# Moving the homes of a decoder trunk's buffers to multiples of 256 bytes

## The chip, the cores and the metric

The kernel runs on one core of a Trainium2 chip as one launch. The metric is the device time of one execution in microseconds (us). Before the change the median of three runs is 948.88 us (948.61 to 949.41). A second set of numbers comes from one profiled execution; its time is 948.47 us, and its trace spans 946.7 us from the first to the last instruction.

## The reference, cut to what matters

One layer of a hybrid decoder on 512 tokens with 1024 channels, all float32: a norm, one input projection that feeds three causal linear-recurrent mixers and their merge gates, an output projection, then a SwiGLU feed-forward part with 2816 hidden channels and a last norm.

```python
proj = jnp.einsum('bld,dp->blp', rmsnorm(x, norm_mix), w_in)
...
o_a = merge_heads(rmsnorm(o_a, gn_a)) * silu(a_g)          # HGRN2, 4 heads of 128
o_b = merge_heads(head_groupnorm(o_b)) * silu(b_g)         # RetNet, 4 heads, rotary q and k
o_c = merge_heads(rmsnorm(o_c, gn_c)) * silu(c_g)          # GLA, 4 heads, low-rank gate
merged = (gates[:, :, 0] * (o_a @ w_br_a) + gates[:, :, 1] * (o_b @ w_br_b)
          + gates[:, :, 2] * (o_c @ w_br_c))
h = x + merged @ w_out
f = (silu(hn @ w_gate) * (hn @ w_up)) @ w_down             # hn = rmsnorm(h, norm_ffn)
return rmsnorm(h + f, norm_final)
```

## The kernel before, in words

Every large product is made three times over in float32r, TensorE's faster reading of float32: each operand is split into a high part (a cast on ScalarE, line 77) and a low part (a subtraction on VectorE, line 78), and TensorE adds high times high, high times low and low times high into the same PSUM bank. Every pass is one matmul of a 128x128 stationary operand (loaded by a LDWEIGHTS just before it) and a 128x512 moving operand. Weights come by DMA, 512 KB at a time, into three rotating buffers `wraw`; their split halves rotate through three `whi` and three `wlo`.

In the program's order the float32r matmuls are these. "Moving" is the operand that streams through the array, "stationary" the one that LDWEIGHTS loads.

| stage | moving | stationary | matmuls of 512 columns |
|---|---|---|---|
| value projections of A and C (`vproj`, L238) | `whi`, `wlo` | `uh`, `ul` | 192 |
| value projection of B (`vproj`, L238) | `whi`, `wlo` | `xh`, `xl` | 96 |
| 52 chunks of the input projection (`proj`, L105 to L107) | `xh`, `xl` | `whi`, `wlo` | 1248 |
| branch projections (L105 to L107) | `oh`, `ol` | `whi`, `wlo` | 288 |
| output projection (`oproj`) | `whi`, `wlo` | `mh`, `ml` | 192 |
| feed-forward up and gate (`product`, L793), seven products in a Strassen scheme, five column blocks of 512 | `whi`, `wlo` | `fh`, `fl` | 841 |
| feed-forward down (`down`), without its tail | `whi`, `wlo` | `dh`, `dl` | 480 |
| the last four row blocks of the second down pass (`tail`) | `tw` | `dh`, `dl` | 48 |

The sixth column block of the feed-forward part has 256 columns: 168 matmuls more of that width (L793). The small products of the mixers (scores, states, transposes; L310 to L365, L401, L473, L619, L806) are plain float32 matmuls, each of which the profile shows as two records.

The order of the work is that of the code; around the mixers a `weave` lets one generator's steps alternate with another's, so that TensorE does chunks of `proj` while VectorE works on a mixer's scores.

Where a buffer lies is set by the pools. Those without a side are laid one after another from the bottom of each partition (`cpool`, `wpool`, `tpool`, then `xpool`, `mpool`, later `xform` and `dpool`); a pool with `side="right"` is laid from the top down (`spool`, later `fw`). `cpool` holds small constants, `wpool` the weight buffers, `tpool` temporaries, `spool` 39 slots of 2048 bytes. Each tile's place is rounded up to 32 bytes. Nothing asks for more: the small tiles at the front and the end of `cpool` and `tpool` shift all that stands behind them.

Of the kernel before, what the change touches and what calls it, by code (L numbers as in the profile page):

```python
# [8 lines left out]
F32 = mybir.dt.float32  # L9
# [6 lines left out]
P = 128  # L16
# [3 lines left out]
WARM = 11  # L20
GAP = 4
TAIL = 4
RATES = (2.0, 1.2, 1.3)
NT = L // P
FFN = 2816
# [24 lines left out]
def trunk_kernel(ctx: ExitStack, tc: tile.TileContext, xT, x, vecs, nfin, w_main, w_v, w_r, w_gk, w_br, w_out, w_gu,  # L50
                 w_gut, w_down, masks, diag, rot, out):
    nc = tc.nc
    cpool = ctx.enter_context(tc.tile_pool(name="cpool", bufs=1))
    wpool = ctx.enter_context(tc.tile_pool(name="wpool", bufs=3))
    tpool = ctx.enter_context(tc.tile_pool(name="tpool", bufs=8))
    late = ExitStack()
    spool = late.enter_context(tc.tile_pool(name="spool", bufs=39, side="right"))
    mix = ExitStack()
    xpool = mix.enter_context(tc.tile_pool(name="xpool", bufs=1))
# [4 lines left out]
    def slot(shape=(P, L), dtype=F32, name="s"):  # L64
        return spool.tile(list(shape), dtype, tag="s", name=name)

    def temp(shape=(P, L), dtype=F32, name="t"):
        return tpool.tile(list(shape), dtype, tag="t", name=name)
# [4 lines left out]
    def psm(shape=(P, L)):  # L73
        return psp.tile(list(shape), F32, tag="pm", name="pm", bufs=4)

    def split(raw, hi, lo):
        a = nc.scalar.copy(hi, raw)  # L77
        b = nc.vector.tensor_tensor(lo, raw, hi.bitcast(F32), op=ALU.subtract)  # L78
        return a.ins, b.ins
# [57 lines left out]
    def col(i):  # L137
        return vec[:, i:i + 1]
# [7 lines left out]

    def rroot(ps, n, r):
        nt = ps.shape[1]
        m = tpool.tile([P, nt], F32, tag="rm", name="rm", bufs=2)
        nc.vector.tensor_scalar(m, ps, 1.0 / n, EPS, op0=ALU.mult, op1=ALU.add)  # L150
        return nc.gpsimd.tensor_tensor(r, m, mhalf[:, :nt], op=ALU.pow)

# [59 lines left out]
    def proj(ch):  # L212
        wh, wl = wload(w_main[ch], KT, P)
        ps = psj()
        for kt in range(KT):
            mm3(ps, wh[:, kt, :], wl[:, kt, :], xn_h[kt], xn_l[kt], kt == 0, kt == KT - 1)
        return ps
# [72 lines left out]
    for h in range(4):  # L290
        k, f = slot(name="ka"), slot(name="fa")
        ps = proj(CH["a_f"] + h)
        s = temp(name="sp")
# [158 lines left out]
    def head_out(pss, gn, gs, o, h0):  # L452

        n = len(pss)
        ss = tpool.tile([P, n * NT], F32, tag="hs", name="hs", bufs=2)
        r = tpool.tile([P, n * NT], F32, tag="hr", name="hr", bufs=2)
        for j, ps in enumerate(pss):
            sq = temp((P, NT, P), name="osq")
            nc.scalar.activation(sq, ps, AF.Square)
            nc.vector.tensor_reduce(ss[:, j * NT:(j + 1) * NT], sq, axis=mybir.AxisListType.X, op=ALU.add)  # L460
        rroot(ss, P, r)
        ons = []
        for j, ps in enumerate(pss):
            on = temp((P, NT, P), name="on")
            nc.vector.tensor_tensor(on, ps, r[:, j * NT:(j + 1) * NT, None].to_broadcast([P, NT, P]), op=ALU.mult)
            ons.append(on)
        for _ in range(GAP):
            yield
        pts = []
        for on in ons:  # L470
            pt = psm()
            for t in range(NT):
                nc.tensor.transpose(pt[:, t * P:(t + 1) * P], on[:, t, :], dg[:, 0, :])  # L473
            pts.append(pt)
        for j, pt in enumerate(pts):
            g = gs[h0 + j]
            if gn is None:
                nc.vector.tensor_tensor(g, g, pt, op=ALU.mult)
            else:
                nc.vector.scalar_tensor_tensor(g, g, gn, pt, op0=ALU.mult, op1=ALU.mult)  # L480
            oh, ol = slot(dtype=F32R, name="oh"), slot(dtype=F32R, name="ol")
            split(g, oh, ol)
            o[h0 + j] = (oh, ol)
        yield

    def mixer_gated(units, vs, gn, gs, o):
        for n, (qs, ks, fs) in enumerate(units):
            pos = []
            yield from gated(qs, ks, fs, vs, 2 * n, pos)
            yield from head_out(pos, gn, gs, o, 2 * n)  # L490
# [30 lines left out]
    def gproj(name, g):  # L521
        for h in range(4):
            g[h] = slot(name="gg")
            nc.scalar.activation(g[h], proj(CH[name] + h), AF.Silu)
            yield
# [44 lines left out]
    def b_in():  # L570
        rt = []
        for j in range(4):
            t = mpool.tile([P, L], F32, tag=f"rot{j}", name="rot", bufs=1)
            nc.sync.dma_start(t, rot[j])
            rt.append(t)
        for n, name in ((0, "b_q"), (2, "b_k")):
            z = []
            for j in range(2):
                ps = proj(CH[name] + j)
                t = temp(name="rz")  # L580
                nc.scalar.copy(t, ps)
                z.append(t)
                yield
            dst = [slot(name="qb") for _ in range(2)]
            for j in range(2):
                a, b, c = temp(name="ra"), temp(name="rb"), temp(name="rc")
                nc.gpsimd.tensor_tensor(a, z[0], rt[n + j], op=ALU.mult)
                nc.vector.tensor_tensor(b, z[1], rt[n + 1 - j], op=ALU.mult)
                nc.vector.tensor_tensor(c, a, b, op=ALU.add if j else ALU.subtract)
                for h in range(4):  # L590
                    r = (h % 2) * 64 + j * 32
                    nc.gpsimd.dma_start(dst[h // 2][r:r + 32, :], c[h * 32:h * 32 + 32, :])
            qk.append(dst)
        for p in vproj(1, xn_h, xn_l):
            if p is not None:
                for t, ps in enumerate(p):
                    s = tpool.tile([P, 4], F32, tag="vsum", name="vsum", bufs=2)
                    nc.vector.tensor_reduce(s, ps.rearrange("p (h v) -> p h v", h=4), axis=mybir.AxisListType.X,
                                            op=ALU.add)
                    nc.vector.tensor_scalar(s, s, -1.0 / P, None, op0=ALU.mult)  # L600
                    v = slot(name="vb")
                    for h in range(4):
                        hs = slice(h * P, (h + 1) * P)
                        nc.scalar.activation(v[:, hs], ps[:, hs], AF.Identity, bias=s[:, h:h + 1])
                    vB.append(v)
            yield
# [19 lines left out]
    def weave(mains, side, rate):  # L626
        acc = 0.0
        done = False
        for g in mains:
            for _ in g:  # L630
                acc += rate
                while acc >= 1.0:
                    acc -= 1.0
                    if not done and next(side, StopIteration) is StopIteration:
                        done = True
        for _ in side:
            pass

    oA, oB, oC = [None] * 4, [None] * 4, [None] * 4
    unitsA = [(qA[2 * n:2 * n + 2], kA[2 * n:2 * n + 2], fA[2 * n:2 * n + 2]) for n in range(2)]  # L640
    weave([gproj("a_g", gA), c_in(), b_in()], mixer_gated(unitsA, vA, col(V_GNA), gA, oA), RATES[0])
    weave([gproj("c_g", gC), gproj("b_g", gB), branch(0, oA, False)], mixer_gated(unitsC, vC, col(V_GNC), gC, oC), RATES[1])
    weave([branch(2, oC, False)], mixer_b(oB), RATES[2])
    for _ in branch(1, oB, True):
# [215 lines left out]
    hs = hnat(0, first_half)  # L860
# [11 lines left out]
    hs = hnat(1, second_half)  # L872
# [41 lines left out]
    def hidden(H, kt):  # L914
        hi = dpool.tile([P, 256], F32R, tag="dh", name="dh", bufs=TAIL + 2)
        lo = dpool.tile([P, 256], F32R, tag="dl", name="dl", bufs=TAIL + 2)
        split(hidT[kt][:, H * 256:(H + 1) * 256], hi, lo)
# [13 lines left out]

    def finish(H, tl, ys):
        t = 2 * H + tl
        m3 = tpool.tile([P, 1], F32, tag="m3", name="m3", bufs=2)
        r3 = tpool.tile([P, 1], F32, tag="r3", name="r3", bufs=2)
        nc.vector.tensor_tensor(m3, ss3[:, t:t + 1], ss3[:, NT + t:NT + t + 1], op=ALU.add)
        rroot(m3, D, r3)
        for c in range(2):
            cs = slice(c * HALF, (c + 1) * HALF)
            nc.vector.scalar_tensor_tensor(ys[c], ys[c], r3, nf[:, cs], op0=ALU.mult, op1=ALU.mult)  # L940
            (nc.scalar if c else nc.sync).dma_start(out[t * P:(t + 1) * P, cs], ys[c])

    for H in range(2):
        bank = (psj, psm)[H]
        ps = [[None] * 2 for _ in range(2)]
        hr = [[None] * 2 for _ in range(2)]
        tail = []
        for kt in range(FT):
            if kt == 8:
                for tl in range(2):  # L950
                    for c in range(2):
                        hr[tl][c] = dpool.tile([P, HALF], F32, tag="hr", name="hr", bufs=4)
                        nc.sync.dma_start(hr[tl][c], hspill[2 * H + tl, c])
            kept = H and kt >= FT - TAIL
            raw = wdma(w_down[kt], D)
            if kept:
                ws = [dpool.tile([P, D], F32R, tag=f"tw{i}", name="tw", bufs=TAIL) for i in range(2)]
                split(raw, *ws)
            else:
                ws = [t[:, 0, :] for t in wsplit(raw, 1, D)]  # L960
            hs = hidden(H, kt)
# [117 lines left out]
```

## Time and profile before

| what | value |
|---|---|
| median of three runs | 948.88 us |
| profiled execution | 948.47 us |
| span of its trace | 946.7 us |
| TensorE busy | 921.7 us, 97% of the span |
| VectorE, ScalarE, GpSimd busy | 561.5, 411.4, 84.0 us |
| mean granted TensorE clock | 0.992 of full speed |

The gap between the time of the profiled execution and its span (1.8 us) lies outside of the first and last instruction. A matmul's own duration in the profile (about 390 ns for 512 columns) overlaps its neighbours', since matmuls are pipelined; how many TensorE finishes in a time is read from the distance between two starts, divided by the number of matmuls between them.

### The profile page before, as it was taken

The numbers are of one execution on the slowest core, as the hardware profiler recorded it, in microseconds if no ns is written. First come the engines' busy times: TensorE is split into PE (matmuls) and PEld (weight loads), VectorE is DVE, ScalarE is ACT, GpSimd is POOL, SyncE is SP. The second block draws the span as 40 slices with busy tenths as digits, with TensorE's granted clock in tenths as the row PEclk, the third lists the DMA queues.
The fourth block names the chain that finished last, engine by engine and source line by source line (L and its number), as shares of the span: only waits on it lengthen the run. The fifth ranks groups of instructions, "written<-read, shape, count | busy, mean of one in ns | idle before, by whom it ended". The sixth has DMA issues, their size and how long they took to land.

```text
span 946.7 us, 11541 instructions
## 1 busy us (share of the span) xinstructions
PE 921.7 (97%) x4476; PEld 751.4 (79%) x4476; DVE 561.5 (59%) x752; ACT 411.4 (43%) x602; POOL 84.0 (9%) x79
## 2 busy tenths in 40 slices
PE   8999999999999999999999996899999999999997
PEld 7888778888878778888888884688888889888885
DVE  7823545766453564444343466897786976656764
ACT  6433328233323223223233466455545555554642
POOL 2101103113000000111222000000000000000000
PEclk9999999999999999999999998899999999999999
DMA  8332211222222222222232563452222321555862
GB/s 285 115 111 89 89 45 43 70 90 89 90 67 67 89 67 68 90 67 67 89 100 100 182 241 111 178 173 95 90 94 84 134 67 45 178 185 194 269 198 89
DMA packets 33239, 108.74 MB, mean 115 GB/s; under 512 B 4096, under 2 KB 4512, under 8 KB 33184
## 3 DMA queue, kind: packets, MB, share of 16 engines
q1 hardware_dynamic: 31456, 103.81, 33.0%
q0 software_dynamic: 1152, 3.15, 1.0%
q10 hardware_dynamic: 576, 1.05, 0.3%
q8 instruction: 35, 0.57, 0.2%
q14 instruction: 20, 0.16, 0.1%
HBM read 102.74 MB, written 4.19 MB: 113 GB/s over the span
## 4 chain that ended last, share of the span: by engine, by line
PE 93%; DVE 3%; ACT 1%; issue 1%; DMA 1%; SPq 0%; DVEq 0%; POOLq 0%; ACTq 0%
PE pj L793 16%; PE pj L105 15%; PE pj L106 15%; PE pj L107 15%; PE pm L793 6%; PE pj L238 5%; PE pm L105 3%; PE pm L107 3%; PE pm L106 3%; PE pm L365 1%; PE pm L362 1%; PE pm L238 1%; PE pm L340 1%; PE pm L343 1%; PE pm L806 1%
## 5 line engine op out<-in xcount | busy, mean ns | idle before, releaser
L78 DVE TENSOR_TENSOR wlo<-wraw,whi 128x1024 fp32r<-128x1024 f32 (+1 forms) x150 | 185.7, 1239 | 212.1 <-ACT whi L77 204.5
L77 ACT CAST whi<-wraw 128x1024 fp32r<-128x1024 f32 (+1 forms) x150 | 156.4, 1043 | 297.8 <-PE pj L106 187.3
L105 PE MATMUL pj<-xh,whi 128*128 128x512 f32 x416 | 167.2, 402 | 0.0
L106 PE MATMUL pj<-xl,whi 128*128 128x512 f32 x416 | 164.8, 396 | 0.0
L107 PE MATMUL pj<-xh,wlo 128*128 128x512 f32 x416 | 164.7, 396 | 0.0
L793 PE MATMUL pj<-whi,fh 128*128 128x512 f32 (+1 forms) x240 | 92.4, 385 | 6.8 <-ACT whi L77 6.7
L793 PE MATMUL pj<-wlo,fh 128*128 128x512 f32 (+1 forms) x240 | 90.9, 380 | 4.8 <-DVE wlo L78 4.8
L107 PEld LDWEIGHTS pj<-xh,wlo 128*128 128x128 f32 x416 | 78.3, 188 | 18.0
L105 PEld LDWEIGHTS pj<-xh,whi 128*128 128x128 f32 x416 | 78.3, 188 | 17.6 <-issue 0.3
L106 PEld LDWEIGHTS pj<-xl,whi 128*128 128x128 f32 x416 | 78.4, 188 | 17.3
L793 PE MATMUL pj<-whi,fl 128*128 128x512 f32 (+1 forms) x240 | 91.5, 381 | 0.0
L78 DVE TENSOR_TENSOR wlo<-wv,whi 128x1024 fp32r<-128x1024 f32 x44 | 53.7, 1223 | 22.2 <-ACT whi L77 21.1
L77 ACT CAST whi<-wv 128x1024 fp32r<-128x1024 f32 x44 | 46.1, 1050 | 46.4 <-PE pj L793 28.4
L793 PEld LDWEIGHTS pj<-whi,fh 128*128 128x128 f32 x240 | 46.0, 192 | 16.5 <-ACT whi L77 7.3
L793 PEld LDWEIGHTS pj<-wlo,fh 128*128 128x128 f32 x240 | 45.9, 191 | 14.4 <-DVE wlo L78 5.5
L793 PEld LDWEIGHTS pj<-whi,fl 128*128 128x128 f32 x240 | 46.1, 192 | 8.8
L105 PE MATMUL pj<-oh,whi 128*128 128x512 f32 x96 | 39.1, 407 | 0.0
L107 PE MATMUL pj<-oh,wlo 128*128 128x512 f32 x96 | 38.1, 397 | 0.0
L77 ACT CAST dh<-hid 128x256 fp32r<-128x256 f32 x44 | 17.4, 406 | 47.4 <-PE pj L106 29.6
L106 PE MATMUL pj<-ol,whi 128*128 128x512 f32 x96 | 37.9, 395 | 0.0
L513 POOL TENSOR_TENSOR mrg<-mrg,mt 128x512 f32<-128x512 f32 x16 | 25.8, 1613 | 123.3 <-DVE mt L512 123.3
L793 PE MATMUL pm<-whi,fh 128*128 128x512 f32 (+1 forms) x96 | 36.5, 380 | 0.0
(257 smaller groups left out, 1605.4 us busy)
## 6 DMA issues: line engine op xcount, KB each, us to landing
wraw<-in_w_main_dram SPq DMA_DIRECT2D x52, 512.0 KB, 3.3
wraw<-in_w_down_dram SPq DMA_DIRECT2D x44, 512.0 KB, 3.5
wr<-in_w_gu_dram SPq DMA_DIRECT2D x25, 512.0 KB, 3.8
wraw<-in_w_out_dram SPq DMA_DIRECT2D x16, 512.0 KB, 3.4
wraw<-in_w_gu_dram SPq DMA_DIRECT2D x15, 512.0 KB, 4.2
wraw<-in_w_br_dram SPq DMA_DIRECT2D x12, 512.0 KB, 3.4
wraw<-in_w_v_dram SPq DMA_DIRECT2D x11, 512.0 KB, 4.4
xraw<-in_xT_dram SPq DMA_DIRECT2D x8, 256.0 KB, 6.2
```

Source lines behind the costliest of these rows:

```text
L77: a = nc.scalar.copy(hi, raw)
L78: b = nc.vector.tensor_tensor(lo, raw, hi.bitcast(F32), op=ALU.subtract)
L105: nc.tensor.matmul(ps, lhsT=ah, rhs=bh, start=start, stop=False)
L106: nc.tensor.matmul(ps, lhsT=ah, rhs=bl, start=False, stop=False)
L107: nc.tensor.matmul(ps, lhsT=al, rhs=bh, start=False, stop=stop)
L238: nc.tensor.matmul(pss[t], lhsT=a[kt][:, t * P:(t + 1) * P], rhs=b[:, k, :], start=kt == 0 and n == 0, stop=kt == KT - 1 and n == 2)
L340: nc.tensor.matmul(ps[:, t, :], lhsT=pa[:, h, t, :], rhs=vs[t][:, hs], start=t == 0, stop=False)
L343: nc.tensor.matmul(ps[:, t, :], lhsT=q, rhs=sts[h % n][r, t - 1, :], start=False, stop=t == NT - 1)
L362: nc.tensor.matmul(out, lhsT=ks[0][:, j], rhs=isel(qs[0]), start=True, stop=True)
L365: nc.tensor.matmul(out[:, h], lhsT=ks[h][:, j], rhs=isel(qs[h]), start=True, stop=True)
L513: nc.gpsimd.tensor_tensor(mrg[dt], mrg[dt], t, op=ALU.add)
L793: nc.tensor.matmul(banks[tl][:, :n], lhsT=x_[:, kt, ts], rhs=w_[:, kk, :], start=start and kt == 0 and q == 0, stop=kt == 3 and q == 2, sk ...
```

## The change

One constant, two padding tiles and six moved tiles. A tile of 56 floats (224 bytes) that nobody reads is put at the top of each partition, ahead of `spool`; a tile of `PAD` = 64 floats (256 bytes) at the front of `cpool`; and six kinds of small tiles (`rm`, `hs`, `hr`, `vsum`, `m3`, `r3`) are taken from `cpool` instead of `tpool`, with as many buffers as before. No instruction is added, removed or moved on any engine, and each waits for the same semaphores as before; only the addresses differ.

```diff
+PAD = 64
...
+    ctx.enter_context(tc.tile_pool(name="edge", bufs=1, side="right")).tile([P, 56], F32, tag="edge", name="edge")
+    cpool.tile([P, PAD], F32, tag="edge", name="edge")
     spool = late.enter_context(tc.tile_pool(name="spool", bufs=39, side="right"))
...
-        m = tpool.tile([P, nt], F32, tag="rm", name="rm", bufs=2)
+        m = cpool.tile([P, nt], F32, tag="rm", name="rm", bufs=2)
...
-        ss = tpool.tile([P, n * NT], F32, tag="hs", name="hs", bufs=2)
-        r = tpool.tile([P, n * NT], F32, tag="hr", name="hr", bufs=2)
+        ss = cpool.tile([P, n * NT], F32, tag="hs", name="hs", bufs=2)
+        r = cpool.tile([P, n * NT], F32, tag="hr", name="hr", bufs=2)
...
-                    s = tpool.tile([P, 4], F32, tag="vsum", name="vsum", bufs=2)
+                    s = cpool.tile([P, 4], F32, tag="vsum", name="vsum", bufs=2)
...
-        m3 = tpool.tile([P, 1], F32, tag="m3", name="m3", bufs=2)
-        r3 = tpool.tile([P, 1], F32, tag="r3", name="r3", bufs=2)
+        m3 = cpool.tile([P, 1], F32, tag="m3", name="m3", bufs=2)
+        r3 = cpool.tile([P, 1], F32, tag="r3", name="r3", bufs=2)
```

The homes that follow from it, in bytes from the start of the partition, taken from the two built programs. What a float32r matmul reads of a buffer starts at a multiple of 512 bytes within it (but for `wr`), so the remainder of the home is that of the operand.

| buffers | first home before | mod 256 | mod 512 | first home after | mod 256 | mod 512 |
|---|---|---|---|---|---|---|
| `whi` (and `wlo`, `wraw`, temporaries) | 33408 | 128 | 128 | 34048 | 0 | 256 |
| `xh`, `xl` | 76800 | 0 | 0 | 77056 | 0 | 256 |
| `fh`, `fl` | 74752 | 0 | 0 | 75008 | 0 | 256 |
| `dh`, `dl` | 78848 | 0 | 0 | 79104 | 0 | 256 |
| `tw` | 99328 | 0 | 0 | 99584 | 0 | 256 |
| slots: `uh`, `ul`, `oh`, `ol`, `mh`, `ml` and others | 149472 | 224 | 480 | 149248 | 0 | 256 |
| `dg` (masks and the identity of the transposes) | 17344 | 192 | 448 | 17600 | 192 | 192 |
| `wr`, `gkw` | 18912, 19936 | 224 | 480 | 19232, 20256 | 32 | 288 |

## Rows read from the trace of the kernel before

**Rows 1.** The page: span; busy time, share, instructions; the chain by engine.
```profile
span 946.7 us, 11541 instructions
...
PE 921.7 (97%) x4476; PEld 751.4 (79%) x4476; DVE 561.5 (59%) x752; ACT 411.4 (43%) x602; POOL 84.0 (9%) x79
...
PE 93%; DVE 3%; ACT 1%; issue 1%; DMA 1%; SPq 0%; DVEq 0%; POOLq 0%; ACTq 0%
```
**Rows 2.** Timeline of TensorE's tail: start us, us, engine line op operands.
```profile
930.04 0.39 PE L105 MATMUL pm<-tw,dh 128*128 128x512 f32 x1
...
938.88 0.39 PE L105 MATMUL pm<-tw,dh 128*128 128x512 f32 x1
```
**Rows 3.** Timeline of TensorE in a pass of the input projection.
```profile
152.24 0.39 PE L106 MATMUL pj<-xl,whi 128*128 128x512 f32 x1
...
162.92 0.40 PE L107 MATMUL pj<-xh,wlo 128*128 128x512 f32 x1
```
**Rows 4.** Timeline of TensorE in the down projection, ahead of the tail.
```profile
897.75 0.39 PE L107 MATMUL pm<-whi,dl 128*128 128x512 f32 x1
...
903.79 0.40 PE L106 MATMUL pm<-wlo,dh 128*128 128x512 f32 x1
```
**Rows 5.** Chain in order of time, feed-forward: start us, us, what.
```profile
643.14 16.73 PE pj L793 x72
...
800.85 8.54 PE pj L793 x72
```
**Rows 6.** Chain, value projections of C and of B.
```profile
46.37 2.81 PE pj L238 x12
...
211.00 11.14 PE pj L238 x48
```
**Rows 7.** Timeline of TensorE, first branch matmul of two neighbouring output blocks.
```profile
498.32 0.40 PE L105 MATMUL pj<-oh,whi 128*128 128x512 f32 x1
...
506.70 0.40 PE L105 MATMUL pj<-oh,whi 128*128 128x512 f32 x1
```
**Rows 8.** Busy time by engine in five stretches.
```profile
core 0: us, PE busy (x) PEld busy (x) DVE busy (x) ACT busy (x) POOL busy (x), PEclk, DMA share, GB/s
16.00:37.00 21.00, 21.00 (x100) 17.24 (x99) 19.44 (x24) 12.36 (x19) 8.56 (x5) 1.00 0.56 193
68.20:71.40 3.20, 3.20 (x15) 2.60 (x14) 0.00 (x0) 0.00 (x0) 0.00 (x0) 1.00 0.52 164
570.00:600.00 30.00, 18.52 (x74) 14.42 (x74) 20.44 (x30) 16.10 (x32) 4.30 (x6) 0.77 0.43 151
586.00:599.70 13.70, 7.25 (x16) 5.32 (x17) 12.58 (x20) 5.89 (x10) 2.13 (x2) 0.50 0.38 132
600.00:700.00 100.00, 99.89 (x446) 80.94 (x445) 81.86 (x79) 56.16 (x69) 0.00 (x0) 1.00 0.36 123
```
**Rows 9.** TensorE's waits: for whom, us in total, times, longest.
```profile
PE pm L365 <- DVE ka L442: 1.4, 2, 0.8
PE pm L362 <- DVE kc L442: 1.3, 4, 0.7
```
**Rows 10.** Chain, two float32 groups of a mixer.
```profile
149.04 0.89 PE pm L340 x8
...
163.32 0.87 PE pm L473 x8
```
**Rows 11.** Groups of VectorE by shape: busy us, mean ns, idle before.
```profile
L78 DVE TENSOR_TENSOR wlo<-wraw,whi 128x1024 fp32r<-128x1024 f32 x148 | 184.3, 1246 | 211.5 <-ACT whi L77 203.9 <-PE pm L806 6.3
...
L78 DVE TENSOR_TENSOR wlo<-wr,whi 128x1024 fp32r<-128x1024 f32 x16 | 19.6, 1223 | 10.7 <-ACT whi L77 10.4
```
**Rows 12.** Timeline of TensorE while VectorE, ScalarE and GpSimd stand still.
```profile
68.40 0.39 PE L107 MATMUL pj<-xh,wlo 128*128 128x512 f32 x1
...
71.20 0.39 PE L107 MATMUL pj<-xh,wlo 128*128 128x512 f32 x1
```

## The prediction

> **What bounds the kernel now.** I read the page first: TensorE is busy for 921.7 of 946.7 us, and 93% of the chain that ended last is TensorE's own work [rows 1]. So nothing that shortens a wait can be worth much; only the pace of the matmuls themselves can. The program's instructions, their order and their waits are the same after the change, so the question is whether an operand's address alters how long an instruction takes.
>
> For that I read the timeline of TensorE, where the distance between two starts, divided by the matmuls between them, gives the pace. The trace holds an experiment on addresses, because the homes of before differ by stage. In the tail, `tw` streams and `dh`, `dl` are loaded, and all of them lie at a multiple of 256: the start goes from 930.04 to 938.88 in 39 steps, which is 226.7 ns for a matmul of 512 columns [rows 2]. Just ahead of it the same `dh` and `dl` are loaded and only the moving operand differs, `whi` or `wlo` at remainder 128: 897.75 to 903.79 in 26 steps, 232.3 ns [rows 4]. In the input projection it is the other way, the moving `xh`, `xl` at 0 and the stationary `whi`, `wlo` at 128: 152.24 to 162.92 in 46 steps, 232.2 ns [rows 3]. With both off (`whi` at 128, `uh` at 224) twelve matmuls take 2.81 us, 234.2 ns each [rows 6]. All of this is at a granted clock of 1.00, the level of 2.4 GHz [rows 8].
>
> So one operand off a multiple of 256 goes with 5.5 ns more, both with 7.5 ns, out of 227. After the change every float32r product of 512 columns is of the tail's kind.
>
> **The change part by part.** The table of stages gives how many matmuls there are of each kind; the tail's 48 have nothing to gain.
> - Value projections of A and C: 192 x (234.2 - 226.7) = 1.44 us [rows 6].
> - Value projection of B: 48 take 11.14 us, 232.1 each; 96 x 5.4 = 0.52 us [rows 6].
> - Input projection: 1248 x (232.2 - 226.7) = 6.86 us [rows 3].
> - Branches: from 498.32 to 506.70 there are 24 matmuls of the projection and 12 of the branch. Less 24 x 232.2 ns, 2.81 us are left for the 12, or 233.9 each; 288 x 7.2 = 2.07 us [rows 7].
> - Output projection: its operands lie like those of the first group (128 and 224), so I take that pace; 192 x 7.5 = 1.44 us.
> - Feed-forward: 72 in 16.73 us, 232.4 each [rows 5]. Of its 841, 16 start between 586.0 and 599.7, where the granted clock is 0.50, the level of 1.2 GHz [rows 8]; there a matmul is slow for another reason, and I count nothing. 825 x 5.7 = 4.70 us.
> - Down projection: 480 x 5.6 = 2.69 us [rows 4].
>
> The sum is 19.7 us. Three kinds of work I cost at nothing. The 168 products of 256 columns go at 8.54 us for 72, 118.6 ns [rows 5]; half of the tail's pace would be 113.3, so the bounds are 0 and 168 x 5.3 = 0.9 us. I take 0, since a part of a matmul's cost that doesn't shrink with its columns would leave no gain. The plain float32 products make up 4476 less 3385 and 168, or 923 records: two groups with other homes show 0.89 and 0.87 us for eight records [rows 10], so the bounds are 0 and 923 x 2.5 ns = 2.3 us. I take 0, because the slower row has one operand at 0 (`pta`) and the quicker one, a transpose, has none there (`dg` at 192, `on` at 128), so it isn't the home that divides them. VectorE's splits of 1024 columns take 1246 ns with all three operands at 128 and 1223 ns with the input at 224 [rows 11]; that is 2%, of either sign for the change, and beside TensorE's work.
>
> Not all of the 19.7 reaches the end, since what TensorE gains ahead of a wait that another engine ends is lost there.
> - Between 16 and 37 us VectorE is busy for 19.44 of 21.00 us [rows 8]. If it sets the pace of the first 72 matmuls, 72 x 7.5 = 0.5 us are lost.
> - In the mixers TensorE waits for VectorE's gate products six times, 2.7 us in all [rows 9]. Ahead of each of them stand 24 to 48 matmuls of the projection, whose gain (0.13 to 0.26 us) only lengthens the wait: 6 x 0.26 = 1.6 us. This also covers steps in which VectorE is now done just in time.
> - In the feed-forward part VectorE is busy for 81.86 of 100 us [rows 8]. With TensorE 2.4% quicker this is 84%, still with room; I take 0.3 us for its tight places.
> - Between 570 and 600 us TensorE is busy for 18.52 of 30 us [rows 8]: a chain of VectorE and ScalarE on the residual, which moves earlier as a whole and keeps its length. The stretch at 1.2 GHz behind it can come out longer or shorter by a few matmuls, some 0.5 us either way.
>
> The gain is 19.7 - 0.5 - 1.6 - 0.3 = 17.3 us. Against the profiled execution's 948.47 us that makes 931.2; the median of the runs is 0.4 us higher, so I forecast 931.6 us.
>
> A rule of the Trainium skill speaks against the whole sum. The page SBUF — State Buffer (Specifications) says that SBUF is organised in lines of 16 bytes and that a penalty is paid for each crossing into a new line; all homes of before are already multiples of 16, so by that rule alone the change would give nothing. The trace has 226.7 beside 232.3 ns at the same stationary operand [rows 2, 4], which lines of 16 bytes do not explain.
>
> **The rivals.**
> 1. *The tail is quick for another reason.* No weights are under way there and the other engines have little to do. Then the change does nothing and the time stays 948.9 us. Against it: from 68.2 to 71.4 us VectorE, ScalarE and GpSimd stand still [rows 8], and TensorE goes from 68.40 to 71.20 in 12 steps, 233.3 ns each [rows 12], no quicker than beside them. The weights' DMAs do run there, at a share of 0.52. The rule on lines ends in the same time as this rival.
> 2. *256 is too small a step, and what counts is a multiple of 512.* In the table of homes every operand that lies at 0 now also lies at a multiple of 512, and every one after the change at remainder 256 of 512. No row of before shows an operand there. In this case the change takes the good homes away: from the first projection at 54 us on, the classes with one operand off become classes with both off, at some 234.0 ns (between 233.9 and 234.2). The price is 1344 x 1.8 ns (projections with `xh`, `xl`) + 825 x 1.6 + 480 x 1.7 + 48 x 7.3 = 2.42 + 1.32 + 0.82 + 0.35 = 4.9 us, and the time 953.8 us. For it: every row fits it as well as it fits a step of 256. Against it only that it asks more than the rows need, since operands at 128 and 224 are off by either rule; so I give it a fifth of the forecast's chance.
> 3. *Only the moving operand's home counts.* Then the input projection, whose moving operand is at 0 already, gains nothing: 931.6 + 6.9 = 938.5 us. It would need another reason for the projection's 232.2 ns [rows 3], and none shows. The Trainium skill's page TensorE: Matmul & The Clock Gate (Step-by-step: what each phase is for) states that TensorE reads its two operands over separate ports, so that loading the next stationary operand takes nothing from the running matmul. By it, this rival is what one would expect; the projection's pace against the tail's disagrees.
>
> **How the numbers follow.** The forecast has a chance of 0.70, the first rival 0.10, the second 0.14, the third 0.06. The likeliest case has its own range: at the quick end nothing is lost and both unknown gains come in full, 948.5 - 19.7 - 0.9 - 2.3 + 0.4 = 926.0; at the slow end twice as much again is lost to VectorE, 937 us. To leave out no more than 2 in 10, the range has to reach over the third and the first rival, to 949.5 us; the second is left out. A measurement of this kernel can tell about 0.2% (1.9 us) from no change: faster is the forecast and the third rival, 0.76; the same is the first, 0.10; slower is the second, 0.14.
>
> **What would show it.** In the new profile, TensorE's pace in the projection, in the feed-forward part and in the down projection should be 226 to 228 ns, as in the tail, and the tail's own pace unchanged. TensorE's busy time should fall by some 19 us, and its waits for VectorE in the mixers grow by 1 to 2 us. The transposes and scores should keep their 109 and 111 ns. Paces of 234 ns everywhere, in the tail too, would show the second rival; a quick pace in the feed-forward part beside 232 ns in the projection, the third; the old paces throughout, the first. The forecast is wrong in its size if the paces fall and VectorE's waits eat more than 6 us.

## The result, and the profile after

The changed kernel takes 932.88 us, the median of four runs (931.29 to 935.10), where the kernel before, run beside it, takes 949.14 us (948.61 to 951.03). The ratio is 0.9827, with a 95% interval of 0.9802 to 0.9851: 16.3 us faster. The forecast was 931.6 us.

The page of the profile after, the lines that answer to [rows 1]:

```profile
span 933.3 us, 11541 instructions
...
PE 907.0 (97%) x4476; PEld 750.5 (80%) x4476; DVE 561.6 (60%) x752; ACT 411.6 (44%) x602; POOL 82.9 (9%) x79
...
PE 90%; DVE 4%; ACT 2%; DMA 2%; issue 1%; SPq 0%; DVEq 0%; POOLq 0%; ACTq 0%
```

TensorE has the same 4476 records and is busy for 14.7 us less; no other engine's busy time moved by more than 1.1 us. So the time came out of the matmuls themselves. TensorE's share of the chain fell from 93% to 90%, and DMA's rose from 1% to 2%: something at the end is late now, and the last rows of this section show it.

Next the timeline of TensorE in the input projection, answering to [rows 3]. The first two rows are 30 matmuls apart. The last three stand behind eight transposes that break the stream.

```profile
155.19 0.39 PE L110 MATMUL pj<-xl,whi 128*128 128x512 f32 x1
...
161.99 0.39 PE L110 MATMUL pj<-xl,whi 128*128 128x512 f32 x1
...
163.55 0.40 PE L110 MATMUL pj<-xl,whi 128*128 128x512 f32 x1
...
164.47 0.39 PE L111 MATMUL pj<-xh,wlo 128*128 128x512 f32 x1
...
168.55 0.39 PE L111 MATMUL pj<-xh,wlo 128*128 128x512 f32 x1
```

6.80 us for 30 matmuls are 226.7 ns, the tail's pace of [rows 2]. But behind the transposes the first four steps take 0.92 us, 230 ns each, and only the next 18 (4.08 us) go at 226.7.

The chain in order of time, for a value projection, a float32 group, the feed-forward part in 512 and in 256 columns, answering to [rows 5, 6, 10]:

```profile
39.78 2.72 PE pm L242 x12
...
148.58 0.89 PE pm L344 x8
...
635.00 16.34 PE pj L797 x72
...
789.30 8.63 PE pj L797 x72
```

12 in 2.72 us are 226.7 ns (234.2 before), and 72 in 16.34 us are 226.9 ns (232.4 before). The products of 256 columns gained nothing: 119.9 ns against 118.6. Nor did the float32 group, 0.89 us as before.

TensorE's timeline in the down projection, answering to [rows 4]; the two rows are 54 steps apart, 12.24 us, again 226.7 ns:

```profile
884.69 0.39 PE L109 MATMUL pm<-whi,dh 128*128 128x512 f32 x1
...
896.93 0.39 PE L109 MATMUL pm<-whi,dh 128*128 128x512 f32 x1
```

TensorE's waits, answering to [rows 9]:

```profile
PE pm L369 <- DVE ka L446: 1.5, 2, 0.9
PE pj L242 <- DVE wlo L82: 1.5, 1, 1.5
PE pm L366 <- DVE kc L446: 1.4, 4, 0.8
...
PE pm L110 <- DVE tw L82: 0.2, 1, 0.2
```

The mixers' waits (`ka`, `kc`) grew from 2.7 to 2.9 us only. The wait for `tw`, the tail's weights, is new.

Busy time by stretch, answering to [rows 8]:

```profile
15.60:19.00 3.40, 3.40 (x10) 2.61 (x9) 3.40 (x7) 3.31 (x7) 0.00 (x0) 0.50 0.98 342
...
570.00:600.00 30.00, 18.47 (x72) 14.20 (x71) 24.35 (x33) 19.98 (x37) 4.10 (x6) 0.72 0.47 166
...
600.00:700.00 100.00, 99.76 (x457) 82.65 (x456) 83.77 (x82) 54.78 (x68) 0.00 (x0) 1.00 0.36 117
```

In the same 100 us TensorE now starts 457 matmuls where it started 446, 2.5% more, at the same granted clock of 1.00. The first row is a disturbance of this one execution: from 15.6 to 19.0 us the granted clock was 0.50, the level of 1.2 GHz, and ten matmuls started. Ahead of that fall TensorE had stood still for 1.5 us, waiting for `wlo` (the second of the waits above), and had then started four matmuls. A second profile of the same kernel (experiment e9 below) has the same wait, 1.47 us long, and kept its clock:

```profile
15.60:19.00 3.40, 3.40 (x17) 2.82 (x16) 3.40 (x7) 3.15 (x7) 0.21 (x1) 1.00 1.04 408
...
570.00:600.00 30.00, 18.44 (x72) 14.01 (x71) 25.39 (x33) 19.82 (x34) 2.40 (x3) 0.77 0.40 145
```

Between 570 and 600 us it has a mean clock of 0.77, as before [rows 8], and the first profile 0.72. So I set the second profile (span 930.5 us) against that of before, stage by stage. "By then" is how much earlier TensorE starts the matmul that ends the stage; the forecast is the sum of the prediction's terms and losses for that stage.

| stage, up to | by then, us | in the stage | forecast |
|---|---|---|---|
| first matmul of the input projection | 0.89 | 0.89 | 0.94 |
| first of the output projection | 8.66 | 7.77 | 7.85 |
| last of the output projection | 9.87 | 1.21 | 1.44 |
| last of the feed-forward part | 14.28 | 4.41 | 4.40 |
| first of the tail | 16.90 | 2.62 | 2.69 |
| last of the tail | 16.18 | -0.72 | 0 |

Two of these agreements are partly chance. In the second profile TensorE starts its first float32r matmul at 5.50 us and before at 6.32, so 0.82 of the first row's 0.89 us was there ahead of the stage, and the value projections of A and C themselves gave 0.07; in e3, e4, e8 and e11 below, whose paces are the same, they gave 0.3 to 1.0. And the feed-forward part gave 3.6 to 4.0 us in those four and 3.7 in the first profile. In the second it had 9 steps of 350 to 500 ns, as matmuls take them at the lower clock, where the others have 13 to 16 and the kernel before has 13. The other rows repeat: 7.8 to 7.9, 1.1 to 1.2 and 2.6 to 2.7 us in all six.

Only the tail has another sign. The end of the chain in the second profile, and the tail's first and last matmul, show why:

```profile
907.47 4.74 DMA wraw<-in_w_down_dram
912.23 1.06 ACT tw L81
913.31 1.24 DVE tw L82
914.59 0.50 PE pm L110
```

```profile
911.75 0.39 PE L109 MATMUL pm<-tw,dh 128*128 128x512 f32 x1
...
923.15 0.39 PE L111 MATMUL pm<-tw,dl 128*128 128x512 f32 x1
```

A block of the tail's weights comes by DMA, is split by ScalarE and VectorE, and only then can TensorE go on. Before, TensorE reached the tail 16.9 us later and found the blocks split; now it is there first. The 47 steps take 11.40 us in the second profile, where they took 10.67 before. How much is lost differs between profiles: in e3, e4 and e8, where TensorE comes as early, they take 10.8 to 10.9 us, with their longest steps at the same place.

### The profile page after: what moved, and what is told of

It reads as the page before. It is cut to its first block, busy times and chain, and to the rows that moved or that the text cites. A ratio compares the mean times of both kernels' runs of the same rounds, so it can differ in the third digit from the quotient of the medians.

```text
span 933.3 us, 11541 instructions
## 1 busy us (share of the span) xinstructions
PE 907.0 (97%) x4476; PEld 750.5 (80%) x4476; DVE 561.6 (60%) x752; ACT 411.6 (44%) x602; POOL 82.9 (9%) x79
## 4 chain that ended last, share of the span: by engine, by line
PE 90%; DVE 4%; ACT 2%; DMA 2%; issue 1%; SPq 0%; DVEq 0%; POOLq 0%; ACTq 0%
PE pj L797 16%; PE pj L109 15%; PE pj L110 15%; PE pj L111 15%; PE pm L797 6%; PE pj L242 5%; PE pm L110 2%; PE pm L109 2%; PE pm L111 2%; PE pm L369 2%; PE pm L366 1%; PE pm L344 1%; PE pm L242 1%; ACT whi L81 1%; DMA wraw<-in_w_down_dram 1%
## 5 line engine op out<-in xcount | busy, mean ns | idle before, releaser
L109 PE MATMUL pj<-xh,whi 128*128 128x512 f32 x416 | 165.2, 397 | 0.0
L110 PE MATMUL pj<-xl,whi 128*128 128x512 f32 x416 | 162.9, 392 | 0.0
L111 PE MATMUL pj<-xh,wlo 128*128 128x512 f32 x416 | 162.7, 391 | 0.0
L797 PE MATMUL pm<-whi,fl 128*128 128x512 f32 (+1 forms) x96 | 35.7, 372 | 0.0
```

The lines of the kernel that those rows point to most:

```text
L109: nc.tensor.matmul(ps, lhsT=ah, rhs=bh, start=start, stop=False)
L110: nc.tensor.matmul(ps, lhsT=ah, rhs=bl, start=False, stop=False)
L111: nc.tensor.matmul(ps, lhsT=al, rhs=bh, start=False, stop=stop)
L797: nc.tensor.matmul(banks[tl][:, :n], lhsT=x_[:, kt, ts], rhs=w_[:, kk, :], start=start and kt == 0 and q == 0, stop=kt == 3 and q == 2, sk ...
```

## The experiments

Two readings of the gain were to be told apart. **Theory A** is the forecast's: each operand has a home of its own that is good (a multiple of 256) or bad. **Theory B** says that only the difference counts, the remainder by 256 of the stationary operand's address less that of the moving one. In the kernel before both fit, since every good operand lay at 0. Differences below are stationary less moving, modulo 256.

The first four kernels vary the two ends of the layout: the padding at the front shifts what lies at the bottom (`whi`, `wlo`, `xh`, `fh`, `dh` and the rest), the tile at the top shifts `spool` (`uh`, `oh`, `mh`).

**e1, the bottom alone.** The top tile is left out, so `uh`, `oh`, `mh` stay at 224.

```diff
-    ctx.enter_context(tc.tile_pool(name="edge", bufs=1, side="right")).tile([P, 56], F32, tag="edge", name="edge")
```

> The change without the 224-byte tile at the top: weights, inputs, hidden parts and tail at remainder 0 of 256, the 39 slots (uh, ul, oh, ol, mh, ml) back at 224. Theory A (each operand's own home counts, multiples of 256 are the good ones): the projection, the feed-forward part and the down projection keep 226.7 to 227.5 ns per matmul; the 672 matmuls with an operand in a slot go at some 232.3 ns, as one operand off did before. Cost 672 x 5 ns = 3.4 us over the change, some 936.3 us. Theory B (only the difference of the two remainders counts): the same stages slow down, to 232 to 234 ns, 936 to 938 us. If the slots' homes don't matter, 932.9 us.

Measured: 936.69 us, ratio 0.9877 (0.9863 to 0.9892). The chain shows a value projection still slow, at 233.3 ns, and the feed-forward part at 226.7:

```profile
46.59 2.80 PE pj L241 x12
...
658.42 10.88 PE pj L796 x48
```

**e2, the top alone.** The kernel before, with only the top tile.

```diff
+    ctx.enter_context(tc.tile_pool(name="edge", bufs=1, side="right")).tile([P, 56], F32, tag="edge", name="edge")
```

> The kernel before with the 224-byte tile at the top alone: the slots at 0, weights still at 128. Theory A: every 512-column matmul now has exactly one operand off (the weights); the 672 with an operand in a slot go from 234 to 232.3 ns, the others stay. Gain 672 x 1.8 ns = 1.2 us, some 947.8 us. Theory B: the two remainders still differ (by 128 instead of 96), so between no change and the same 1.2 us. If the two homes added up independently, the 672 would gain 5 ns each, 945.6 us.

Measured: 947.66 us, ratio 0.9990 (0.9981 to 1.0000). All pairs with a weight buffer now differ by 128 (the tail's agree, as before), and they go at about one pace: 232.5 ns in the value projection, 232.4 in the feed-forward part:

```profile
46.66 2.79 PE pj L239 x12
...
642.59 16.73 PE pj L794 x72
```

By the medians the bottom alone gives 12.3 us and the top alone 1.3, together 13.6, against 16.3 for the whole change. The parts don't add up, since a pair of a bottom and a top operand (the value projections, branches and output projection) becomes quick only with both shifts. e1 and e2 don't tell the theories apart: Theory A forecast 936.3 and 947.8 us, and Theory B much the same.

**e3, everything at 128.** No operand lies at a multiple of 256, but all have the same remainder.

```diff
-PAD = 64
+PAD = 32
...
-... side="right")).tile([P, 56], F32, tag="edge", name="edge")
+... side="right")).tile([P, 88], F32, tag="edge", name="edge")
```

> PAD = 32 floats and a top tile of 88 floats: every operand of the large matmuls lies at remainder 128 of 256, moving and stationary alike. Theory A: both operands off, 234 ns everywhere, the tail too: 3385 x 7 ns = 24 us over the change, some 954 to 957 us. Theory B: equal remainders, so 226.7 to 227.5 ns everywhere and 932.9 us.

Measured: 932.86 us, ratio 0.9838 (0.9822 to 0.9855), the whole gain of the change:

```profile
45.91 2.72 PE pj L242 x12
...
654.68 10.88 PE pj L797 x48
```

Theory A, which forecast 954 to 957 us, falls here, and with it the forecast's reading of its own rows: a home of 128 is as good as one of 0, provided both operands have it.

**e4, everything at a multiple of 512.** The padding goes, and the top tile becomes longer.

```diff
-... side="right")).tile([P, 56], F32, tag="edge", name="edge")
-    cpool.tile([P, PAD], F32, tag="edge", name="edge")
+... side="right")).tile([P, 120], F32, tag="edge", name="edge")
```

> No pad at the front and a top tile of 120 floats: every operand of the large matmuls lies at remainder 0 of 512 (after the change it is 256 of 512). Theory A (256 is the step): the same 226.7 to 227.5 ns, 932.9 us within 0.2%. If a step of 512 counted beside 256, the pace would fall below 226.7 ns; 5 ns more would be 17 us, 916 us.

Measured: 932.30 us, ratio 0.9834 (0.9819 to 0.9849), with 48 feed-forward matmuls in the same 10.88 us:

```profile
654.55 10.88 PE pj L796 x48
```

The larger step gives nothing more, so the prediction's second rival has no ground on this side either.

**e5 and e6, other differences.** The three `whi` and three `wlo` become buffers a, b, c at 32, 64 and 256 bytes (e5) or 96, 160 and 192 (e6) from the other operands; gap tiles set the distance. `homes()`, not shown, hands out the buffers in turn; its gap tiles have 8, 8, 48, 72, 8, 48 and 64 floats in e5.

```diff
-        hi = wpool.tile([P, 1024], F32R, tag="whi", name="whi", bufs=3)
-        lo = wpool.tile([P, 1024], F32R, tag="wlo", name="wlo", bufs=3)
+        hi, lo = homes()
...
```

> After the change, but the three buffers of whi and of wlo (named whia, whib, whic and wloa, wlob, wloc, in turn) lie 32, 64 and 256 bytes (mod 512) from the remainder of all other operands. One look at the paces in the projection (weights stationary) and in the feed-forward and down parts (weights moving). Theory B with a step of 256: a and b slow, 232 to 234 ns, c at 226.7 to 227.5. Theory B with a step of 512: all three slow. Theory A is already refuted; it would keep c quick too. Time some 2/3 of the gain lost: 944 us by the first, 951 us by the second.

> The same with 96, 160 and 192 bytes between the weights' buffers and all other operands. Theory B with a step of 256: all three slow, at 232 to 234 ns in every stage, 948 to 951 us. If the sign of the difference counts (192 apart being 64 short of the next step), the projection and the feed-forward part would differ at the same buffer, since moving and stationary operand change places; if only its size to the next multiple counts, 192 goes like 64 and 160 like 96.

Measured, one run each: 945.31 us (e5) and 949.28 us (e6), beside 948.51 us for the kernel before. e5's timeline in the input projection, buffers a, b and c in turn, 15, 18 and 9 steps:

```profile
152.30 0.40 PE L121 MATMUL pj<-xh,whia 128*128 128x512 f32 x1
...
155.80 0.40 PE L121 MATMUL pj<-xh,whia 128*128 128x512 f32 x1
...
157.21 0.40 PE L121 MATMUL pj<-xh,whib 128*128 128x512 f32 x1
...
161.41 0.40 PE L121 MATMUL pj<-xh,whib 128*128 128x512 f32 x1
...
165.71 0.39 PE L121 MATMUL pj<-xh,whic 128*128 128x512 f32 x1
...
167.75 0.39 PE L121 MATMUL pj<-xh,whic 128*128 128x512 f32 x1
```

These are 233.3, 233.3 and 226.7 ns: 32 bytes apart is already bad, 256 apart is good. The last holds for the settled pace only. By the mean distance of starts, c takes 228.1 ns in the projection and 229.3 in the feed-forward part, and the timeline of that part shows why, from the first matmul of c behind one of b to the first of a behind c:

```profile
649.91 0.39 PE L808 MATMUL pj<-whic,fh 128*128 128x512 f32 x1
...
651.07 0.39 PE L808 MATMUL pj<-wloc,fh 128*128 128x512 f32 x1
...
652.66 0.40 PE L808 MATMUL pj<-whia,fh 128*128 128x512 f32 x1
```

The first five steps take 1.16 us, 232 ns each, though every pair in them is a good one; the next seven take 1.59 us, 227 each. So what went before counts too: the quick pace comes some steps behind the last bad pair.

The sign counts as well. In the feed-forward part of e5 the buffers are the moving operand, and b gives 229.5 ns there (mean distance of starts inside the class), between the two paces. In e6 buffer c does it in the other place, as the stationary operand of the input projection:

```profile
163.85 0.40 PE L121 MATMUL pj<-xh,whic 128*128 128x512 f32 x1
...
167.98 0.39 PE L121 MATMUL pj<-xh,whic 128*128 128x512 f32 x1
```

18 steps in 4.13 us are 229.4 ns. Both are a difference of 192. Put together, with the mean distance of starts in each class (distances under 300 ns):

| difference | pace, ns, and where |
|---|---|
| 0 | 226.9 feed-forward after, 226.8 down after; 256 apart: 228.1 projection e5 c, 229.3 feed-forward e5 c (settled 226.7 and 227) |
| 32 | 233.1 projection e5 a |
| 64 | 233.4 projection e5 b, 232.9 feed-forward e6 c |
| 96 | 234.2 value projection before, 234.2 projection e6 a, 233.5 feed-forward e6 b |
| 128 | 232.7 projection before, 232.4 feed-forward before |
| 160 | 233.5 branches before, 233.5 projection e6 b, 233.4 feed-forward e6 a |
| 192 | 229.2 projection e6 c, 229.5 feed-forward e5 b |
| 224 | 233.3 value projection e1, 233.5 feed-forward e5 a |

Apart from c's first steps, each difference gives about the same pace in whichever stage and whichever role the shifted buffer has. What the prediction called "both off" was a difference of 96 or 160.

**e7, the low half off.** In the feed-forward part two stationary operands alternate; here `fl` is moved by 128 against `fh`. The two gaps also move both by 256 in every second of the seven products.

```diff
+        xform.tile([P, 32], F32, tag=f"a{name}", name="gap")
...
+        xform.tile([P, 32], F32, tag=f"b{name}", name="gap")
```

> After the change, but each fl (the low half of the feed-forward's stationary operand) lies 128 bytes apart from fh, whi and wlo. The passes run fh-whi, fl-whi, fh-wlo. Theory B1 (the stationary operand that is loaded while a matmul streams, that is the next one's, has to agree with it): the interval that begins with fh-whi is slow, the other two quick. Theory B2 (a matmul's own two operands have to agree): the interval that begins with fl-whi is slow. In either case the part's mean pace rises by about a third of 5.5 ns, 825 x 1.8 = 1.5 us in all, 934.4 us, and the other stages stay.

Measured, one run: 934.44 us, beside 948.51 for the kernel before. The timeline of the feed-forward part:

```profile
634.05 0.40 PE L799 MATMUL pj<-whi,fh 128*128 128x512 f32 x1
634.29 0.40 PE L799 MATMUL pj<-whi,fl 128*128 128x512 f32 x1
634.52 0.39 PE L799 MATMUL pj<-wlo,fh 128*128 128x512 f32 x1
...
636.83 0.40 PE L799 MATMUL pj<-whi,fh 128*128 128x512 f32 x1
```

12 steps take 2.78 us, 231.7 ns. Over the whole stage the distance behind a `whi,fh` is 232.5 ns, behind a `whi,fl` 234.0, behind a `wlo,fh` 227.0 (227.1 in the products where `whi` and `fh` agree modulo 512, 227.0 where they are 256 apart). Only the third has a good stationary operand and a good one coming next. So neither the matmul's own stationary operand nor the next one alone explains it: either one makes the distance long, or a bad pair has an effect beyond its own distance, as e5's buffer c shows that it can. The time met its forecast by luck: the part's mean pace was to rise by 1.8 ns and rose by 4.3, from 226.9 to 231.2.

**e8, the small operands too.** `dg`, `wr` and `gkw`, operands of plain float32 matmuls and splits, are moved to multiples of 256 as well.

```diff
-    cpool.tile([P, PAD], F32, tag="edge", name="edge")
+    cpool.tile([P, 16], F32, tag="edge1", name="edge")
...
+    cpool.tile([P, 40], F32, tag="edge2", name="edge")
...
+    cpool.tile([P, 8], F32, tag="edge3", name="edge")
```

> The change, and the three operands that it leaves out put at remainder 0 of 256 as well: dg (the masks and the identity of the transposes, 192 after the change), wr and gkw (32). If plain float32 matmuls don't depend on the homes, transposes and scores keep their 109 and 111 ns and the time stays at 932.9 us within 0.2%. If they do, each of the some 250 transposes' records gains up to 5 ns, 1.3 us: 931.6 us.

Measured: 932.27 us, ratio 0.9827 (0.9813 to 0.9840); the change itself, on the same chip, 932.21. A group of eight transposes through `dg` keeps its 0.87 us:

```profile
665.33 0.87 PE pm L812 x8
```

So the transposes don't depend on the home of `dg`. For `wr` and `gkw` there is only the time, whose spread is wider than what they could give.

**e9, the change once more**, without an edit, to see whether its slow start belongs to it.

> The changed kernel as it is, for a second profile and more times on the same chip. If the slow start of its first profile (the granted clock at 0.50 from 15.6 to 19.0 us of the trace's own time, TensorE 2.2 us behind the kernel before at 21 us) is chance, this profile starts like that of the kernel before and its span is some 931 us; if it belongs to the change, it comes again and the span is 933 us.

Measured: 932.21 us, ratio 0.9822 (0.9808 to 0.9835), the granted clock 1.00 from 15.6 to 19.0 us (shown above). The slow start doesn't belong to the change, and cost the first profile 2.2 of the 2.8 us by which its span is longer.

**e10, `wlo` alone off by 128**, to separate the two readings that e7 left.

```diff
+        wpool.tile([P, 32], F32, tag="gap", name="gap", bufs=1) if not gaps else None
...
+        wpool.tile([P, 32], F32, tag="gap2", name="gap", bufs=1) if len(gaps) == 1 else None
```

> After the change, but wlo lies 128 bytes apart from all other operands (modulo 256). In the feed-forward and down parts wlo is the moving operand of one pass in three, and the stationary operands all agree with each other. Theory B3 (a matmul is slow if its moving operand differs from its own stationary one or from the one loaded while it streams): there only the interval that begins with the wlo matmul is slow, the other two stay at 227 ns. If a slow interval instead comes from a change and is followed by a second one (what e7 showed as two in three), that interval and the next are slow. In the projection, where wlo is the stationary operand of one pass in three, both give two slow intervals in three, as in e7. Mean pace 228.5 to 229 (B3) or 231 ns in the feed-forward part, 231 ns in the projection; 941 us by B3, 943.5 us by the other.

Measured, one run: 946.49 us, beside 949.91 for the kernel before. The chain of a value projection and of the feed-forward part:

```profile
46.16 2.80 PE pj L247 x12
...
641.34 16.80 PE pj L802 x72
```

72 in 16.80 us are 233.3 ns, slower than the kernel before (232.4), though only one pass of three has a bad pair. The distances are 230.1 ns behind `whi,fh`, 235.5 behind `whi,fl` and 233.8 behind `wlo,fh`; both readings wanted less, in the paces and in the time. The edit also put `whi` 256 away from `fh`, `xh` and `dh`, but that isn't the cause: in the value projections of A and C, where `whi` and `uh` still agree, the three distances are 229.9, 235.8 and 233.8 ns. A rule that neither reading named fits more: a distance is long where the matmul's own pair or the next one's is off. It fits e7, and here the feed-forward part and the projection (227.5 behind `xh,whi`, 232.3 behind `xl,whi`, 233.6 behind `xh,wlo`). It fails in the down projection, where the passes run `whi,dh`, `wlo,dh`, `whi,dl`: the distance behind `whi,dl`, which the rule calls quick, is the longest, 233.0 ns, against 230.8 behind `whi,dh` and 229.6 behind `wlo,dh`. No rule by pairs alone was found that fits both, and the question stays open.

**e11, the tail's weights early.** The first of the tail's blocks is fetched into a buffer of its own, long before the tail.

```diff
-            raw = wdma(w_down[kt], D)
+            if H and kt == 12:
+                pre = dpool.tile([P, D], F32, tag="pre", name="pre")
+                nc.sync.dma_start(pre, w_down[FT - TAIL])
+            raw = pre if H and kt == FT - TAIL else wdma(w_down[kt], D)
```

> The changed kernel, with the weights of the first tail block loaded earlier into a buffer of their own, so that the three tail loads behind it each come one buffer sooner. If the wait of TensorE in the tail (0.4 to 0.6 us for the split tw, whose weights land 4.3 to 4.8 us after their issue) is what took the tail's share of the gain, that wait goes and the time falls by 0.4 to 0.7 us, to 931.6 us; if it only moves to another load, the time stays at 932.2 us.

Measured: 931.82 us, ratio 0.9825 (0.9811 to 0.9838). The timeline of the tail, its first and last matmul:

```profile
912.06 0.39 PE L109 MATMUL pm<-tw,dh 128*128 128x512 f32 x1
...
922.71 0.39 PE L111 MATMUL pm<-tw,dl 128*128 128x512 f32 x1
```

The 47 steps take 10.65 us, 226.6 ns each, and the wait for `tw` is gone. In the second profile of the change they took 11.40 us. The 0.7 us are back in the trace; between the medians (931.82 against 932.21 and 932.88) they can't be told from the spread. Part of the 0.7 is the second profile's own, since e3, e4 and e8 lose 0.1 to 0.3 us there without this edit. It is the lowest median of the study, level with the change.

## Why the prediction was right, and where its reasons were not

**TensorE's pace bounds the kernel: right.** The waits barely moved, TensorE's busy time fell by 14.7 us in the first profile and 17.8 in the second (903.9 us), where the prediction wanted some 19, and the time by 16.3.

**The terms of the sum: right in total, some mis-sized.** The prediction multiplied settled paces. By the mean distances inside each class the gain per matmul was 5.2 ns in the input projection (232.7 to 227.5; forecast 5.5), 5.1 in the branches (233.5 to 228.4; forecast 7.2), 6.0 in the output projection (233.9 to 227.9; forecast 7.5), 5.5 in the feed-forward part (5.7) and 5.5 in down (5.6). The branch term is the one most off: 288 x 5.1 = 1.5 us, not 2.07. The value projections of A and C went from 234.2 to 227.7, but of the 0.94 us that was to be left there after the loss to VectorE the stage itself gave 0.07: TensorE's waits in it grew from 1.2 to 1.9 us, for `wlo` and `uh`. The 0.89 us by then is chance, as said above.

**The loss of 1.6 us to VectorE in the mixers: right in size, wrong in its cause.** The waits of [rows 9] grew by 0.2 us. By the class means the terms of that stage are 1248 x 5.2 + 96 x 5.2 + 288 x 5.1 = 8.5 us and not 9.45, so 0.9 us of the missing 1.6 is the pace itself: behind a break the first steps go at some 230 ns also after the change, and the branches gain less. The other 0.7 us is that the class means hold for 1498 of the stage's 1632 matmuls; the 134 that stand next to a break gained 0.1 us together in the second profile, the 0.2 us of longer waits included. An overestimate of the gain and an overestimate of the waits met, and that the stage came out within 0.1 us of its forecast is no merit of either.

**The feed-forward part: right in its pace, and within its margin only at times.** 4.41 us came in the second profile against 4.40 forecast, which is the highest of six profiles: the others show 3.6 to 4.0. The prediction had allowed 0.5 us either way for the stretch at the lower clock.

**The tail, taken as unchanged: wrong by 0.1 to 0.7 us.** Its pace didn't change, but the wait that the prediction should have asked for, what is late once TensorE comes 17 us earlier, was the DMA of its weights. The prediction looked for tight places at VectorE alone. e11 bears this out in one profile: with one block fetched early, the wait is gone and the tail takes 10.65 us, as before the change.

**The work costed at nothing: right.** 256 columns went from 118.6 to 119.9 ns, which over 168 is 0.2 us lost. The float32 groups kept 0.89 and 0.87 us, and e8 gave `dg` a multiple of 256 without effect on the transposes. (The count of 923 holds 17 float32r matmuls, 16 of `wr` and one of the feed-forward part; the bound falls by less than 0.1 us.)

**The reading of the rows: wrong.** The prediction inferred a good and a bad home for each operand, and a price for one or two bad ones. [rows 2 to 4] only compare pairs, and a pair at 0 and 0 can't tell "both at a multiple" from "both alike". e3 told them apart. The forecast was right because the change made all pairs alike, which serves either reading; for e3 the same reading was off by more than 20 us. (The granted clock was 1.00 in all the stretches that the prediction compares, also in those that [rows 8] leave out.)

**The rivals.** The first (the tail is quick for another reason) fell with the pace of every stage. The second (a step of 512) fell with the same paces, and e4 and e5's buffer c confirm it. The third (only the moving operand) fell with the projection, whose moving operand stayed at remainder 0 of 256 and which went from 232.7 to 227.5 ns. The Trainium skill's page TensorE: Matmul & The Clock Gate (Step-by-step: what each phase is for), by which the load of the next stationary operand takes nothing from the running matmul, leaves no reason why the place of the stationary operand should matter. This trace shows that it does: e5's buffers change that place alone in the projection, which goes at 233.3 or 226.7 ns. By the Trainium skill's page SBUF — State Buffer (Specifications) and its lines of 16 bytes, 32 apart would be as good as 0; e5's buffer a, at 233.3 ns, doesn't agree with that.

**What stays open** is the mechanism: whether the matmul's own stationary operand or the next one's counts (e7, e10), why the quick pace comes only some steps behind the last bad pair (e5), and why a difference of 192 costs less than half as much as one of 64. The experiments show that the difference of the homes sets the pace, not how.

## What to carry to other kernels

Where a kernel is bound by TensorE and each matmul loads a stationary operand of its own, look at where the two operands lie in their partition: here equal remainders by 256 bytes were worth 2 to 3% of the pace, at no instruction. A pair of rows shows the effect of a pair; before reading a rule for each operand into it, find or make the case where both are shifted alike. And when the bounding engine becomes quicker everywhere, follow it to the end and ask which transfer it will meet there.

## What the runs showed of the hardware that was not expected

- The pace of a float32r matmul of 512 columns depends on the difference of its operands' addresses modulo 256, not on either address: 226.7 ns settled at a difference of 0, with both at remainder 0, at 128 or at 256 of 512, 232 to 234 ns at 32, 64, 96, 128, 160 and 224, and 229 to 230 ns at 192.
- The quick pace takes some matmuls to set in: 230 ns over four steps behind transposes, 232 over five behind matmuls of a bad pair (e5), then 226.7 to 227.
- With one of three pairs bad, more than one distance grows (feed-forward part, e7: 232.5, 234.0, 227.0 ns; e10: 230.1, 235.5, 233.8), and by more in all than that pair's share of the loss.
- The same kernel had a granted clock of 0.50 from 15.6 to 19.0 us in one profile and of 1.00 in another, after almost the same wait (1.49 and 1.47 us).
